# Transposing the gated values of narrow expert slots on VectorE, and moving the wide slot beside slots of two groups

## The chip, the cores and the metric

The kernel runs on one core of a Trainium2 chip. The time is device microseconds (us) of one execution of the whole program; the numbers compared are medians of several runs. TensorE (PE in the profile) multiplies, VectorE (DVE) and ScalarE (ACT) work on elements, SyncE (SP) starts the DMA transfers that bring the weights from the chip's memory.

## The reference, cut to what matters

Two layers of an encoder trunk on 256 tokens of width 1024, in float32. The second layer ends in a mixture of eight experts, each a gated two-layer network of inner width 3584, of which every token uses two:

```python
def swiglu(h, w_gate, w_up, w_down):
    return (jax.nn.silu(h @ w_gate) * (h @ w_up)) @ w_down

def moe_swiglu(h, w_router, b_router, w_gate, w_up, w_down):
    ...
    top_val, top_idx = lax.top_k(logits, TOP_K)
    top_w = jax.nn.softmax(top_val, axis=-1)
    ...
    for e in range(N_EXPERTS):
        out = out + combine[:, e:e + 1] * swiglu(t, w_gate[e], w_up[e], w_down[e])
```

The change lies in these experts alone. Everything ahead of them (the first layer, and the attention and convolution of the second) is the same program in both kernels.

## The kernel before, in words

**Slots.** Expert 0 has slot 0; the other seven experts are sorted by how many tokens chose them, and slots 1 to 7 take them in that order. A slot has room for a fixed number of groups of 32 tokens, `CAPS`: 3, 4, 3, 3, 3, 2, 2, 2. Slot 1, with four groups (128 tokens), is called wide, the others narrow. Tokens that find no room would be worked off by `rest` behind the end, a loop that runs only if there are any.

**Units.** Each slot goes through its expert's inner width in seven chunks of 512. One chunk of one slot is a unit: `gu_mm` multiplies the slot's tokens with the chunk's gate and up weights into `ps_gu`, ScalarE and VectorE form `mh` = silu(gate) * up (lines 1120 and 1123), `h_T` transposes `mh` to `hT`, and `dn_mm` multiplies it with the chunk's down weights, adding to the slot's `ps_d`. The transposition is there because the down product sums over the inner width, which must lie across partitions.

**Order.** Slots stand in two lanes, `LANES`, and units alternate between them; lane 0 starts three units ahead (`STAGGER`). The order is written out by hand under `tc.manual_schedule()`: each engine gets its instructions in the order in which the loop over `units` issues them. For unit n the loop issues `gu_mm` of unit n, then `dn_mm` of unit n-1 (`pend`), then `h_T` of unit n, so that `hT` is read only after the next unit's gate and up product. When a slot ends, `gated` and `combine` add its result to `macc`; two units ahead of a slot's start, `slot_pick` and `dispatch` gather its tokens (`ps_g`, `ps_w`).

**Narrow and wide.** A narrow unit multiplies in plain float32 straight from the loaded weights: for each group four products of 32 rows run beside each other in TensorE's columns (`streams`, line 1089). The wide unit splits each loaded half of a chunk into an upper and a lower part, `hi` on ScalarE (line 140) and `lo` on VectorE (line 148), and makes three products for each (`mm3`, lines 254 to 256). The splits are issued by `ahead`, some units before they are used.

**Loads and buffers.** A unit loads six transfers of 1024 KB (`load`, line 131): four of gate and up weights, two of down weights. They go through SyncE's queue in the order of `plan`, and each waits until its buffer has been read. The pool `raw` has nine buffers of this size. Where no wide chunk is near in the plan, the three `hi` and three `lo` buffers serve as load buffers too (in `need`), fifteen in all:

```python
if i >= first_gu and not any(n_ for _, n_ in plan[i - 6:i + 3]):
    at = m % 15
    return ((rawp, "raw", G), (hip, "hi", G), (lop, "lo", G))[(at >= 9) + (at >= 12)]
return rawp, "raw", G
```

Of the kernel before, what the change touches and what calls it, by code (L numbers as in the profile page):

```python
# [9 lines left out]
F32 = mybir.dt.float32  # L10
F32R = mybir.dt.float32r
I32 = mybir.dt.int32
U32 = mybir.dt.uint32
AF = mybir.ActivationFunctionType
ALU = mybir.AluOpType
AX = mybir.AxisListType

P = 128
# [16 lines left out]
SPARE4 = (1, 6, 8)  # L35
EARLY = 7
CAPS = (3, 4, 3, 3, 3, 2, 2, 2)
LANES = (0, 2, 1, 3), (5, 4, 6, 7)
STAGGER = 3
NR = NE - 1  # L40
EPS = 1e-6
# [12 lines left out]
def kernel(ctx, tc, x, cvec, wada, bada, wga, wqkv, wout, wfgu, wfd, wfd2,  # L54
                      wmgu, wmd, cols, bias, wrt, brt, out):
    nc = tc.nc
# [10 lines left out]
    def bank(name):  # L67
        return pb.tile([P, 512], F32, tag="b", name=name)

    def accbank(name):  # L70
        return pacc.tile([P, 512], F32, tag="acc", name=name)
# [3 lines left out]
    def sized(tag):  # L75
        def f(name, shape, dt=F32):
            return pools["wk"].tile(shape, dt, tag=tag, name=name, bufs=bufs[tag])
        return f

    a8, a4, a2 = sized("a8"), sized("a4"), sized("a2")  # L80
# [23 lines left out]
    ident = const.tile([P, P], F32, name="ident")  # L104
# [17 lines left out]
    def load(ap, n=4096, mk=lambda s: (rawp, "raw", G)):  # L122

        raw = []
        for h in range(n // G):
            src = ap[h] if isinstance(ap, list) else ap[:, h * G:h * G + G]
            pool, tag, w = mk(h)
            raw.append([])
            for o_ in range(0, G, w):
                r = pool.tile([P, w], F32, tag=tag, name="raw", bufs=bufs.get(tag))  # L130
                nc.sync.dma_start(r, src[:, o_:o_ + w])
                raw[-1].append(r)
        return raw
# [29 lines left out]
    first_gu = len(plan)  # L163
    runs = [[(e, c) for e in lane for c in range(N_DN)] for lane in LANES]
    units = runs[0][:STAGGER]
    for u in zip(runs[0][STAGGER:], runs[1]):
        units += u
    units += runs[1][-STAGGER:]
    after = {e: n for lane in LANES for e, n in zip(lane, lane[1:])}
    order = {0: 0}  # L170
# [736 lines left out]
    def moe(acc, g_bc, mm, A, B, AW, bw):  # L907
# [95 lines left out]
        def pick(col, n=P):  # L1003

            pm = a2("pm", [P, 2, NT, P])
            for t in range(NT):
                nc.vector.tensor_scalar(pm[:, 1, t, 0:n], iota_f[:, 0:n], col(t), y[t], op0=ALU.is_equal,
                                        op1=ALU.mult)
            for t in range(NT):
                nc.vector.tensor_scalar(pm[:, 0, t, 0:n], iota_f[:, 0:n], col(t), None, op0=ALU.is_equal)  # L1010
            return pm
# [5 lines left out]
        def gather(pm, n, put):  # L1017

            for q in range(2):
                ps = bank("ps_g").rearrange("p (j s) -> p j s", j=4)  # L1020
                f = a2("xf", [P, 4, P])
                for j in range(4):
                    k = 4 * q + j
                    for t in range(NT):
                        nc.tensor.matmul(ps[:, j, 0:n], x_sb[:, t, k * P:(k + 1) * P], pm[:, 1, t, 0:n],  # L1025
                                         start=t == 0, stop=t == NT - 1)
                for j in range(4):
                    k = 4 * q + j
                    nc.scalar.activation(f[:, j, 0:n], ps[:, j, 0:n], AF.Identity, scale=A[:, k:k + 1],
                                         bias=B[:, k:k + 1])  # L1030
                put(slice(4 * q, 4 * q + 4), f[:, :, 0:n])
# [93 lines left out]
            return hm  # L1125

        def h_T(hm, g, split=False):
            ps = bank("ps_hT").rearrange("p (a s) -> p a s", a=4)
            for t in range(g):
                nc.tensor.transpose(ps[:, t, :], hm[:, t, :], ident)  # L1130
            if split:
                hT = [a2(n, [P, g, P], F32R) for n in ("hThi", "hTlo")]
                nc.scalar.activation(hT[0], ps, AF.Copy)
                nc.vector.tensor_tensor(hT[1], ps, hT[0].bitcast(F32), op=ALU.subtract)
            else:
                hT = a2("hT", [P, g, P])
                nc.scalar.activation(hT, ps[:, 0:g, :], AF.Copy)  # L1137
            return hT

        def dn_mm(e, c, hT):  # L1140
# [67 lines left out]
        def rest(e):  # L1208

            pm = pick(lambda t: posm[:, t, 0:1])  # L1210
            xg = a8("xr", [P, KT, P])
            gather(pm, P, lambda js, f: nc.scalar.activation(xg[:, js, :], f, AF.Copy))
            ps = bank("ps_w")
            for t in range(NT):
                nc.tensor.transpose(ps[:, t * P:(t + 1) * P], pm[:, 0, t, :], ident)
            for t in range(NT):
                nc.tensor.matmul(ps[:, 2 * P:2 * P + 1], pm[:, 0, t, :], comb[:, t, 0:1], start=t == 0,
                                 stop=t == NT - 1)
            pT = a2("pmT", [P, NT, P])
            nc.scalar.activation(pT.rearrange("p t s -> p (t s)"), ps[:, 0:2 * P], AF.Copy)  # L1220
            ws = sm.tile([P, 1], F32, tag="ws", name="ws")
            nc.vector.tensor_copy(ws, ps[:, 2 * P:2 * P + 1])
            acc = [accbank(f"ps_x{hf}") for hf in range(2)]

            def own(w, c):
                return [r for r, in load(w[bass.ds(e, 1), c].rearrange("o p n -> (o p) n"))]

            for c in range(N_DN):
                pss = [bank(f"ps_gr{b}") for b in range(2)]
                for b in range(2):  # L1230
                    for s, r in enumerate(own(wmgu, 2 * c + b)):
                        for i in range(4):
                            k = 4 * s + i
                            nc.tensor.matmul(pss[b], xg[:, k, :], r[:, 512 * i:512 * i + 512], start=k == 0,
                                             stop=k == KT - 1)
                hm = a2("mh", [P, 4, P])
                for b in range(2):
                    v = pss[b].rearrange("p (u j s) -> p j u s", j=2, u=2)
                    sg = a2("sg", [P, 2, P])
                    nc.scalar.activation(sg, v[:, :, 0, :], AF.Silu)  # L1240
                    nc.vector.tensor_tensor(hm[:, 2 * b:2 * b + 2, :], v[:, :, 1, :], sg, op=ALU.mult)
                hT = h_T(hm, 4)
                for hf, r in enumerate(own(wmd, c)):
                    for k in range(4):
                        nc.tensor.matmul(acc[hf], hT[:, k, :], r[:, 512 * k:512 * k + 512], start=c == 0 and k == 0,
                                         stop=c == N_DN - 1 and k == 3)
            for hf in range(2):
                sl = slice(hf * 512, hf * 512 + 512)
                f = a4("yg", [P, 512])
                nc.vector.scalar_tensor_tensor(f, acc[hf], ws, g2_bc[:, sl], op0=ALU.mult, op1=ALU.mult)  # L1250
                for t in range(NT):
                    ps = bank("ps_sc")
                    nc.tensor.matmul(ps, pT[:, t, :], f, start=True, stop=True)
                    nc.vector.tensor_tensor(macc[:, t, sl], macc[:, t, sl], ps, op=ALU.add)
            for v in (posm, comb):
                nx = sm.tile([P, NT, NE], F32, tag="nx", name="nx", bufs=2)
                nc.vector.tensor_copy(nx[:, :, 0:NE - 1], v[:, :, 1:NE])
                nc.vector.tensor_copy(nx[:, :, NE - 1:NE], v[:, :, 0:1])
                nc.vector.tensor_copy(v, nx)
# [33 lines left out]
        with tc.manual_schedule():  # L1293
# [6 lines left out]
            for n, (e, c) in enumerate(units):  # L1300
# [4 lines left out]
                elif n == STAGGER - 1:  # L1305
                    nxt = LANES[1][0]
                else:
# [8 lines left out]
                hm = gu_mm(e, between)  # L1316
                if n == 1:
# [5 lines left out]
                    ps = bank("ps_g2")  # L1323
# [15 lines left out]
                if n + 1 < len(units) and wide(units[n + 1][0]):  # L1339
                    ahead(2)  # L1340
                pend = e, c, h_T(hm, CAPS[e], wide(e))
                if nxt is not None:
                    disp[nxt] = dispatch(nxt, pm)
# [8 lines left out]
        with tc.If(over > 0):  # L1352
            nc.vector.tensor_tensor(posm, posm, own_room[:, None, :].to_broadcast([P, NT, NE]), op=ALU.subtract)
            for again in range(2):
                with tc.For_i(0, NE, 1) as e:
                    rest(e)
                nc.vector.tensor_scalar(posm, posm, float(-P), None, op0=ALU.add)
            for hf in range(2):
                store(hf)
# [152 lines left out]
```

## Time and profile before

| what | value |
|---|---|
| three runs | 1418.91, 1425.69, 1429.92 us (median 1425.69) |
| the profiled execution | 1421.24 us, its span 1419.2 us |
| TensorE, matmul | busy 1349.9 us, 95% of the span |
| VectorE, ScalarE | busy 565.3 us (40%) and 398.4 us (28%) |
| granted TensorE clock, mean | 0.987 |
| memory read | 470.01 MB, 332 GB/s over the span |

The span is from the first to the last instruction of the profiled execution. Shares of busy time are means over stages that differ: from 519 us on the experts run, and everything else stands ahead of that. In the windows below, one row is one stretch of time; its last number is the rate at which the weights arrived.

### The profile page before, as it was taken

What the parts mean: (1) busy time and instruction counts of PE and PEld (TensorE: products, weight loads), DVE (VectorE), ACT (ScalarE), POOL (GpSimd) and SP (SyncE); (2) the same over time, 40 slices, a digit from 0 to 9 for tenths busy, and PEclk for the clock granted to TensorE, in tenths of its full rate; (3) what the DMA queues carried; (4) which work ended last, traced back from release to release, by engine and by line L of the source; (5) the groups of instructions that cost most, each with busy time, mean ns of one, the idle gap of its engine ahead of it and who ended that gap; (6) DMA issues with size and microseconds to landing.
All of it is one profiled execution on the core that took longest, in us unless ns stands there. A gap on an engine that the chain in (4) does not pass through costs nothing.

```text
span 1419.2 us, 38942 instructions
## 1 busy us (share of the span) xinstructions
PE 1349.9 (95%) x17604; PEld 973.1 (69%) x17604; DVE 565.3 (40%) x1025; ACT 398.4 (28%) x635; POOL 3.0 (0%) x17
## 2 busy tenths in 40 slices
PE   4998899999899999999999999999999999999886
PEld 4877699999697686657666656677667766665453
DVE  3597677777689651000100100354455430010011
ACT  3335444433456330101001001334333420100000
POOL 0000000000000000000000000000000000000000
PEclk9999999999999999999999999999999999999998
DMA  9963787878551579899999995989898999999995
GB/s 383 418 243 123 263 308 273 305 272 307 172 205 45 206 292 369 342 417 417 417 417 417 417 417 223 396 350 362 327 379 346 397 417 417 417 417 417 417 418 202
DMA packets 66379, 473.64 MB, mean 334 GB/s; under 512 B 7840, under 2 KB 7968, under 8 KB 9248
## 3 DMA queue, kind: packets, MB, share of 16 engines
q1 hardware_dynamic: 66208, 471.09, 83.3%
q8 instruction: 140, 2.29, 0.6%
q14 instruction: 31, 0.25, 0.0%
HBM read 470.01 MB, written 1.05 MB: 332 GB/s over the span
## 4 chain that ended last, share of the span: by engine, by line
PE 77%; DMA 13%; DVE 5%; ACT 3%; issue 1%; SPq 0%; DVEq 0%; ACTq 0%
PE ps_gu L1089 23%; PE ps_d L1089 13%; DMA raw<-in_wmgu 6%; DMA raw<-in_wmd 6%; PE ps_ga L256 4%; PE ps_ga L254 4%; PE ps_ga L255 4%; PE ps_g L1025 2%; PE ps_y L708 2%; PE ps_gu L256 2%; PE ps_gu L254 2%; PE ps_gu L255 2%; DVE cv L544 2%; PE ps_ada L308 1%; DVE lo L148 1%; PE ps_hT L1130 1%
## 5 line engine op out<-in xcount | busy, mean ns | idle before, releaser
L1089 PE MATMUL ps_gu<-raw,xn 128*32 128x256 f32 x8064 | 450.2, 380 | 4.1 <-DMA raw<-in_wmgu 3.9
L1089 PEld LDWEIGHTS ps_gu<-raw,xn 128*32 128x32 f32 x8064 | 269.1, 110 | 169.2 <-DMA raw<-in_wmgu 7.8
L148 DVE TENSOR_TENSOR lo<-raw,hi 128x2048 fp32r<-128x2048 f32 x99 | 225.5, 2289 | 84.7 <-ACT hi L140 82.0
L1123 DVE TENSOR_TENSOR mh<-ps_gu,sg 128x256 f32<-128x256 f32 (+1 forms) x91 | 32.7, 382 | 547.2 <-ACT sg L1120 547.2
L1089 PE MATMUL ps_d<-raw,hT 128*32 128x256 f32 x4032 | 232.3, 381 | 8.0 <-DMA raw<-in_wmd 7.5
L140 ACT ACTIVATE hi<-raw 128x2048 fp32r<-128x2048 f32 x99 | 188.3, 1912 | 107.2 <-PE ps_ga L256 43.0
L1089 PEld LDWEIGHTS ps_d<-raw,hT 128*32 128x32 f32 x4032 | 133.7, 110 | 96.6 <-DMA raw<-in_wmd 9.9
L1120 ACT ACTIVATE sg<-ps_gu 128x256 f32<-128x256 f32 (+1 forms) x91 | 32.0, 352 | 426.3 <-PE ps_gu L1089 380.7
L254 PE MATMUL ps_ga<-hThi,lo 128*128 128x256 f32 x480 | 137.5, 287 | 7.6 <-ACT hThi L446 7.6
L256 PE MATMUL ps_ga<-hTlo,hi 128*128 128x256 f32 x480 | 136.9, 285 | 0.8 <-DVE hTlo L451 0.8
L255 PE MATMUL ps_ga<-hThi,hi 128*128 128x256 f32 x480 | 136.3, 284 | 0.0
L254 PEld LDWEIGHTS ps_ga<-hThi,lo 128*128 128x128 f32 x480 | 92.9, 194 | 8.7 <-ACT hThi L446 8.4
L256 PEld LDWEIGHTS ps_ga<-hTlo,hi 128*128 128x128 f32 x480 | 92.4, 192 | 1.4 <-DVE hTlo L451 1.4
L255 PEld LDWEIGHTS ps_ga<-hThi,hi 128*128 128x128 f32 x480 | 92.4, 193 | 0.2
L544 DVE SCALAR_TENSOR_TENSOR cv<-zp,cols_sb,cv 128x256 f32<-128x256 f32 x206 | 85.4, 477 | 0.0
L1137 ACT ACTIVATE hT<-ps_hT 128x384 f32<-128x384 f32 (+1 forms) x49 | 21.8, 445 | 221.4 <-PE ps_hT L1130 221.4
L347 DVE SCALAR_TENSOR_TENSOR ada_acc<-raw,cs,ada_acc 128x512 f32<-128x512 f32 x63 | 47.2, 749 | 1.2
L256 PE MATMUL ps_gu<-lo,xg 128*128 128x512 f32 x112 | 44.3, 396 | 1.3 <-DVE lo L148 1.3
L254 PE MATMUL ps_gu<-hi,xg 128*128 128x512 f32 x112 | 44.8, 400 | 0.0
L255 PE MATMUL ps_gu<-hi,xg 128*128 128x512 f32 x112 | 44.3, 396 | 0.0
L308 PE MATMUL ps_ada<-raw,crep 128*32 128x128 f32 x960 | 34.4, 302 | 7.4 <-DMA raw<-in_wada 7.1
L308 PEld LDWEIGHTS ps_ada<-raw,crep 128*32 128x32 f32 x960 | 29.2, 121 | 11.2 <-issue 8.3
(263 smaller groups left out, 1310.1 us busy)
## 6 DMA issues: line engine op xcount, KB each, us to landing
raw<-in_wmgu SPq DMA_DIRECT2D x222, 1024.0 KB, 13.9
raw<-in_wmd SPq DMA_DIRECT2D x111, 1024.0 KB, 14.3
raw<-in_wada SPq DMA_DIRECT2D x48, 1024.0 KB, 6.2
raw<-in_wfgu SPq DMA_DIRECT2D x22, 1024.0 KB, 6.0
raw<-in_wqkv SPq DMA_DIRECT2D x12, 1024.0 KB, 6.6
raw<-in_wfd SPq DMA_DIRECT2D x11, 1024.0 KB, 6.5
raw<-in_wga SPq DMA_DIRECT2D x8, 1024.0 KB, 10.6
raw<-in_wout SPq DMA_DIRECT2D x8, 1024.0 KB, 7.7
```

Source lines behind the costliest of these rows:

```text
L140: nc.scalar.activation(hi[:, i * w:(i + 1) * w], r, AF.Copy)
L148: nc.vector.tensor_tensor(lo[:, w], r, hi[:, w].bitcast(F32), op=ALU.subtract)
L254: nc.tensor.matmul(o_, a[1], b[0], start=first, stop=False)
L255: nc.tensor.matmul(o_, a[0], b[0], start=False, stop=False)
L256: nc.tensor.matmul(o_, a[0], b[1], start=False, stop=last)
L308: nc.tensor.matmul(ps[32 * g:32 * g + 32, 0:P], crep[:, j, :], w(j)[:, g * P:(g + 1) * P], start=j == 0, stop=j == KT - 1)
L347: nc.vector.scalar_tensor_tensor(accs[ch], ws[ch](j), cs[:, j:j + 1], accs[ch], op0=ALU.mult, op1=ALU.add)
L544: nc.vector.scalar_tensor_tensor(cv[:, a, :], zp[:, a, i:i + S], cw[:, a, i:i + 1], cv[:, a, :], op0=ALU.mult, op1=ALU.add)
L708: nc.tensor.matmul(acc[t][hf], yf[:, k, t * P:(t + 1) * P], w(k // 2, 2 * (k % 2) + hf), start=k == 0, stop=False)
L1089: nc.tensor.matmul(ps[t // 2][32 * j:32 * j + 32, t % 2], x(t), w(j), start=first and t % 2 == 0, stop=last, skip_group_check=True)
L1120: nc.scalar.activation(sg[:, 2 * b:2 * b + m, :], v[:, 0:m, 0, :], AF.Silu)
L1123: nc.vector.tensor_tensor(hm[:, 2 * b:2 * b + m, :], v[:, 0:m, 1, :], sg[:, 2 * b:2 * b + m, :], op=ALU.mult)
```

## The change: what it does

```diff
-LANES = (0, 2, 1, 3), (5, 4, 6, 7)
+LANES = (0, 1, 2, 3), (5, 6, 4, 7)
...
         def h_T(hm, g, split=False):
+            if not split:
+
+                hT = a2("hT", [P, g, 4, 32])
+                v = hm.rearrange("p t (q s) -> p t q s", q=4)
+                for q in range(4):
+                    for j in range(4):
+                        nc.vector.transpose(hT[32 * q:32 * q + 32, :, j], v[32 * j:32 * j + 32, :, q])
+                return hT.rearrange("p t j s -> p t (j s)")
             ps = bank("ps_hT").rearrange("p (a s) -> p a s", a=4)
             for t in range(g):
                 nc.tensor.transpose(ps[:, t, :], hm[:, t, :], ident)
-            if split:
-                hT = [a2(n, [P, g, P], F32R) for n in ("hThi", "hTlo")]
-                nc.scalar.activation(hT[0], ps, AF.Copy)
-                nc.vector.tensor_tensor(hT[1], ps, hT[0].bitcast(F32), op=ALU.subtract)
-            else:
-                hT = a2("hT", [P, g, P])
-                nc.scalar.activation(hT, ps[:, 0:g, :], AF.Copy)
+            hT = [a2(n, [P, g, P], F32R) for n in ("hThi", "hTlo")]
+            nc.scalar.activation(hT[0], ps, AF.Copy)
+            nc.vector.tensor_tensor(hT[1], ps, hT[0].bitcast(F32), op=ALU.subtract)
             return hT
```

In the narrow units, the two or three transposes on TensorE and ScalarE's copy out of PSUM go. In their place VectorE transposes each group's 128x128 values as sixteen blocks of 32x32: block (j, q) goes from partitions 32j to partitions 32q, one instruction for all groups of the slot, so sixteen instructions a unit whether it has two groups or three. The wide slot keeps its transposes on TensorE. `rest` gets the old transposes written out in its own body. The lanes become 0, 1, 2, 3 and 5, 6, 4, 7: slot 1 follows slot 0 and runs beside the end of slot 5 and the beginning of slot 6; slots 2, 3 and 4 come later.

TensorE, two narrow units (slot 5's down product on `ps_d_6035` or `ps_d_6091`, then the next unit of slot 5), before:

```order
L1089 MATMUL ps_gu_5924<-raw,xn 32x256 x4
L1089 MATMUL ps_d_6035<-raw,hT 32x256 x32
L1130 MATMUL ps_hT<-ident,mh 128x128 x3
L1089 MATMUL ps_gu_6078<-raw,xn 32x256 x64
L1089 MATMUL ps_d_5319<-raw,hT 32x256 x8
```

and with the change:

```order
L1089 MATMUL ps_gu_5980<-raw,xn 32x256 x4
L1089 MATMUL ps_d_6091<-raw,hT 32x256 x32
L1089 MATMUL ps_gu_6145<-raw,xn 32x256 x64
L1089 MATMUL ps_d_5330<-raw,hT 32x256 x8
L1089 MATMUL ps_d_5331<-raw,hT 32x256 x4
```

The three transposes between one unit's down product and the next unit's gate and up product are gone. VectorE in a pair of a narrow and a wide unit (`lo` are the splits, `mh` the gated values, `hTlo` the wide unit's), before:

```order
L148 TENSOR_TENSOR lo<-raw,hi 128x2048 x2
L1123 TENSOR_TENSOR mh<-ps_gu_9548,sg 128x256
L1123 TENSOR_TENSOR mh<-ps_gu_9549,sg 128x128
L148 TENSOR_TENSOR lo<-raw,hi 128x2048 x4
L1123 TENSOR_TENSOR mh<-ps_gu_9708,sg 128x256
L1123 TENSOR_TENSOR mh<-ps_gu_9709,sg 128x256
L1134 TENSOR_TENSOR hTlo<-ps_hT,hThi 128x512
```

and with the change, where the narrow slot has two groups:

```order
L148 TENSOR_TENSOR lo<-raw,hi 128x2048 x2
L1123 TENSOR_TENSOR mh<-ps_gu_7150,sg 128x256
L148 TENSOR_TENSOR lo<-raw,hi 128x2048 x2
L1134 STREAM_TRANSPOSE hT<-mh 32x2x32 x16
L148 TENSOR_TENSOR lo<-raw,hi 128x2048 x2
L1123 TENSOR_TENSOR mh<-ps_gu_7286,sg 128x256
L1123 TENSOR_TENSOR mh<-ps_gu_7287,sg 128x256
L1141 TENSOR_TENSOR hTlo<-ps_hT,hThi 128x512
```

The sixteen transposes stand between the splits of the wide unit's first two halves and those of its last two. ScalarE at such a pair, before (beside slot 6):

```order
L140 ACTIVATE hi<-raw 128x2048 x2
L1120 ACTIVATE sg<-ps_gu_10695 128x256
L1120 ACTIVATE sg<-ps_gu_10696 128x256
L1133 ACTIVATE hThi<-ps_hT 128x512
L140 ACTIVATE hi<-raw 128x2048 x2
L1120 ACTIVATE sg<-ps_gu_10817 128x256
L140 ACTIVATE hi<-raw 128x2048 x2
L1137 ACTIVATE hT<-ps_hT 128x256
L140 ACTIVATE hi<-raw 128x2048 x2
L1120 ACTIVATE sg<-ps_gu_10944 128x256
```

and with the change:

```order
L140 ACTIVATE hi<-raw 128x2048 x2
L1120 ACTIVATE sg<-ps_gu_7150 128x256
L140 ACTIVATE hi<-raw 128x2048 x4
L1120 ACTIVATE sg<-ps_gu_7286 128x256
L1120 ACTIVATE sg<-ps_gu_7287 128x256
L1140 ACTIVATE hThi<-ps_hT 128x512
```

The copy `hT` no longer stands between the splits.

## Rows read from the trace of the kernel before

**Rows 1.** The page: the chain that ended last, its line by engine.

```profile
PE 77%; DMA 13%; DVE 5%; ACT 3%; issue 1%; SPq 0%; DVEq 0%; ACTq 0%
```

**Rows 2.** Windows: us, busy us of PE, PEld, DVE, ACT, POOL; PEclk, DMA share, GB/s.

```profile
519.00:588.00 69.00, 67.10 (x1178) 48.50 (x1178) 11.09 (x46) 10.23 (x25) 0.00 (x0) 1.00 0.89 358
588.00:858.00 270.00, 270.00 (x4903) 169.33 (x4902) 22.93 (x62) 27.14 (x70) 0.00 (x0) 1.00 1.01 416
858.00:900.00 42.00, 42.00 (x729) 26.49 (x732) 2.72 (x7) 6.92 (x18) 0.00 (x0) 1.00 0.64 250
900.00:932.00 32.00, 30.66 (x391) 21.03 (x385) 15.00 (x16) 10.27 (x11) 0.00 (x0) 1.00 0.85 336
932.00:1048.00 116.00, 114.54 (x1352) 79.90 (x1340) 56.21 (x49) 50.85 (x51) 0.00 (x0) 1.00 0.90 359
1048.00:1136.00 88.00, 88.00 (x833) 65.97 (x833) 44.94 (x37) 36.85 (x38) 0.00 (x0) 0.96 0.94 379
1136.00:1209.00 73.00, 73.00 (x1171) 45.54 (x1168) 13.96 (x22) 11.17 (x20) 0.00 (x0) 1.00 1.01 417
1209.00:1398.00 189.00, 177.72 (x3090) 103.73 (x3089) 15.72 (x35) 14.84 (x37) 0.00 (x0) 0.99 1.01 414
```

**Rows 3.** The chain in order of time, end of the program: start us, us, what.

```profile
1377.01 21.23 DMA raw<-in_wmd
...
1402.83 4.20 PE ps_d L1089 x64
```

**Rows 4.** The chain, one pair of narrow units (slots 0 and 5).

```profile
600.92 10.50 PE ps_gu L1089 x192
611.42 3.45 PE ps_d L1089 x64
614.87 0.48 PE ps_hT L1130 x3
615.35 7.04 PE ps_gu L1089 x128
...
627.94 2.06 PE ps_gu L1089 x33
```

**Rows 5.** SyncE timeline before the wide slot: start us, us, what.

```profile
852.59 31.02 SPq L131 DMA_DIRECT2D raw<-in_wmgu  x4
...
889.04 10.73 SPq L131 DMA_DIRECT2D raw<-in_wmgu  x4
```

**Rows 6.** The chain, a wide unit beside a three-group unit.

```profile
925.76 5.32 PE ps_d L1089 x96
...
959.50 5.32 PE ps_d L1089 x96
```

**Rows 7.** The chain, a wide unit beside a two-group unit.

```profile
1069.91 3.59 PE ps_d L1089 x64
...
1098.36 3.59 PE ps_d L1089 x64
```

**Rows 8.** VectorE timeline in a wide unit: start us, us, what, [idle before].

```profile
946.94 2.29 DVE L148 TENSOR_TENSOR lo<-raw,hi 128x2048 fp32r<-128x2048 f32 x1 [0.27 <-ACT hi L140]
950.67 4.50 DVE L148 TENSOR_TENSOR lo<-raw,hi 128x2048 fp32r<-128x2048 f32 x2 [1.45 <-ACT hi L140]
```

**Rows 9.** TensorE timeline in the same unit: its first matmul.

```profile
948.06 0.48 PE L254 MATMUL ps_gu<-hi,xg 128*128 128x512 f32 x1
```

**Rows 10.** VectorE timeline: simple operations issued back to back.

```profile
966.68 0.53 DVE L1007 TENSOR_SCALAR pm<-iota_f,rt,ny 128x64 f32<-128x64 f32 x2
967.12 0.41 DVE L1010 TENSOR_SCALAR pm<-iota_f,rt 128x64 f32<-128x64 f32 x2
```

**Rows 11.** VectorE groups of one shape each, 519 to 1411 us.

```profile
L1007 DVE TENSOR_SCALAR pm<-iota_f,rt,ny 128x96 f32<-128x96 f32 x6 | 1.7, 324 | 0.0
```

**Rows 12.** TensorE timeline: a wait and what followed.

```profile
1047.97 0.50 PE L1195 MATMUL ps_sc<-yhi,pmT 32*128 32x256 f32 x3 [1.46 <-DVE mh L1123]
```

**Rows 13.** Window with the granted clock after that wait.

```profile
1050.00:1056.00 6.00, 6.00 (x15) 4.65 (x15) 3.49 (x3) 0.78 (x1) 0.00 (x0) 0.53 1.01 426
```

More of the change, by code (lines that the diff above doesn't have):

```diff
@@ L1241, in rest @@
                     nc.vector.tensor_tensor(hm[:, 2 * b:2 * b + 2, :], v[:, :, 1, :], sg, op=ALU.mult)
-                hT = h_T(hm, 4)
+                ps = bank("ps_hT").rearrange("p (a s) -> p a s", a=4)
+                for k in range(4):
+                    nc.tensor.transpose(ps[:, k, :], hm[:, k, :], ident)
+                hT = a2("hT", [P, 4, P])
+                nc.scalar.activation(hT, ps, AF.Copy)
                 for hf, r in enumerate(own(wmd, c)):
```

## The prediction

> **What bounds the kernel now.** I read the page's chain first. It gives TensorE 77% and transfers 13% [rows 1], which looks like a kernel that any saving on TensorE would shorten. But that is a share over stages, so I went on to the windows over the expert stage, and there the column to follow is the last one. From 1209 to 1398 us, the weights arrive at 414 GB/s with a DMA share of 1.01, while TensorE is busy for 177.7 of 189 us [rows 2]. The end of the chain agrees: it passes through a down-weight transfer up to 1398 us, then a last down product of 4.2 us, and the output [rows 3]. The last 200 us are paced by the weight stream. In such a kernel an early microsecond counts only if it lets the stream run when it would have stood still. So I take 414 GB/s as what the stream can do and read from each window how much of it was lost, as length times (414 minus its rate) over 414 [rows 2]:
>
> 519 to 588 us: 69 x 56/414 = 9.3 us; 858 to 900: 42 x 164/414 = 16.6; 900 to 932: 32 x 78/414 = 6.0; 932 to 1048: 116 x 55/414 = 15.4; 1048 to 1136: 88 x 35/414 = 7.4. That is 54.7 us. The windows 588 to 858 and 1136 to 1209, at 416 and 417 GB/s, give back 1.3 and 0.5. So about **53 us** of stream time are lost, and this is all that the change can win in the expert stage; from the last load's arrival on, nothing changes.
>
> **Why the stream stands still.** One unit loads six transfers of 1024 KB, 6.29 MB. At 414 GB/s a transfer takes 2.53 us and a pair of units 30.4 us. Where TensorE needs longer for a pair, the buffers fill and the loads wait; where it needs less, it eats the lead.
>
> - A pair of slots 0 and 5 (three and two groups) takes 600.92 to 627.94 us, 27.0 us [rows 4]: under 30.4.
> - A wide unit beside a three-group unit takes 925.76 to 959.50 us, 33.7 us [rows 6]: 3.3 us over, in the three pairs where slot 1 stands beside slot 4.
> - A wide unit beside a two-group unit takes 1069.91 to 1098.36 us, 28.4 us [rows 7]: under.
> - Just ahead of the wide slot, four loads take SyncE 31.0 us, against 10.7 a little later [rows 5]. Narrow units can use fifteen buffers, and near wide units only nine are left, so a lead of six transfers, 15.2 us of the stream, must be eaten first. Slots 2 and 4, three groups each, run just before it and let the lead fill up. This is the 16.6 us of the window 858 to 900.
>
> **The reordering.** Slot 1 now begins when slot 0 ends, at the twelfth unit instead of the 26th, and stands beside slots 5 and 6 only, two groups each. All seven of its pairs are of the 28.4 us kind. Ahead of it run four pairs of slots 0 and 5, which eat lead (below, 4.2 us each, 17 us in all, or nearly seven transfers), so there is little to shed at the switch. The three-group slots 2, 3 and 4 move behind the wide slot and meet in pairs (2 with 4, 4 with 3) of 2 x (10.5 + 1.5 x 3.45) = 31.4 us without transposes [rows 4], close to the stream's 30.4. No load is added, and their count on SyncE's queue is the same.
>
> **The transposes on TensorE.** A narrow unit loses three or two of them, with 0.48 us on the chain for three [rows 4]; two thirds of it, 0.32, is my estimate for two. A pair of slots 0 and 5 falls from 27.0 to 26.2 us. Where the stream is the limit this buys nothing: it only moves TensorE's idle time. It helps in the first three units, 3 x 0.48 = 1.4 us, and in the pairs of three-group units. ScalarE also loses the copy that stood between two weight splits and waited until TensorE had got to the transposes.
>
> **The sixteen on VectorE.** No row shows this operation. The nearest rows are simple operations of 64 and 96 columns: two follow each other in 0.44 us, 0.22 each, the next two in 0.41 with their end, so some 0.16 apart [rows 10]; one alone of 96 columns lasts 0.324 us [rows 11]. I take 0.22 because issue one behind another is what sixteen independent ones will do; the bounds are 0.16 and 0.32. Nothing bounds an unseen operation from above with certainty, so a dearer one is a rival. Sixteen then take 3.5 us (2.6 to 5.2). Beside narrow neighbours this hides: the product that reads them is issued after the other lane's down product and a further gate/up product, 3.45 + 7.04 = 10.5 us at least [rows 4], and VectorE is busy for 22.9 of 270 us there [rows 2].
>
> Beside the wide slot it doesn't hide by itself. VectorE's queue holds, between the splits for the wide unit's first two halves and those for its last two, the sixteen transposes, and TensorE waits for the latter. In the unit at 948.06 us [rows 9] the third half's first product comes 24 products later. The 48 of the unit end at 959.50 us, where the next down product starts [rows 6], so they are 11.4/48 = 0.24 us apart, and the third half begins at 953.8 us; its first product on a lower part is the third, at 954.2. The split it needs is ready at 950.67 + 2.25 = 952.9, so there are 1.3 us of slack, and VectorE had been idle for 1.45 us before it [rows 8]. Of 3.5 us therefore 3.5 - 1.45 - 1.3 = 0.8 us become a wait of TensorE. The pair: 28.4 less 0.2 for two transposes, plus 0.8, is **29.0 us**, still under 30.4. Up to 0.31 us a transpose the stream covers it; past that each further 0.1 us costs 1.6 us a pair, 11 us over seven pairs.
>
> A page of the Trainium skill speaks against this step: VectorE: DVE Perf Modes, "The three transpose paths" and the rules behind it, advise TensorE for a 128x128 transpose and name VectorE's 32x32 blocks useful for some layouts only, with 311 ns for a 128x128 tile of bf16. No run here shows that figure. If each of the sixteen cost as much, the sum would stand at the very edge of what the stream covers, and hardly change.
>
> **What remains lost.** In the first window 9.3 - 1.4, 8 us. At the switch I keep the 6.0 us of the window 900 to 932 (the first wide unit beside slot 0's combine) and 6 of the 16.6, since one of the nine buffers comes free only when its own turn has been read, however empty the others are: 12 us (bounds 0 and 22.6). In the seven wide pairs 1 us each for splits that hold a buffer, 7 us (0 to 14). Together 27 of 53, so the **gain is 26 us** (bounds 8 and 45).
>
> The profiled execution took 1421.24 us, with 1419.2 of span; minus 26 it is 1395. It lies 4.4 us under the median of the three runs, 1425.69, and against that the forecast is **1400 us**.
>
> **Rivals.**
>
> - *Transposes of 0.35 to 0.5 us.* VectorE then binds the wide pairs. At 0.42 us, 0.11 too dear, 12 of the 26 us are gone: 1412. For it: 32 partitions are used by each, and I know no row for it. Against: all rows of this size are under 0.33 us [rows 10, 11].
> - *Slower.* The same place, much dearer: at 0.7 us sixteen take 11.2, a wide pair 28.2 + 11.2 - 2.75 = 36.7 us, 6.3 over the stream, 44 over seven pairs, less 26: 1444. The gain is used up at 0.31 + 26/112 = 0.54 us, and it decides by over 1% from 0.67. Beside narrow units 11.2 us would also pass the cover of 10.5.
> - *The clock.* After a wait of 1.46 us [rows 12] the granted clock fell to 0.53 for 1050 to 1056 us [rows 13], mostly the lower of its two levels (1.2 for 2.4 GHz), which lost 6 x 0.47 = 2.8 us. With a stream-bound TensorE there are more such waits. One drop in each wide pair makes 31.8 us of 29.0, 1.4 over the stream, 10 in all: 1410. Against: in 200 us of a stream-bound tail the clock is 0.99 [rows 2]. (The Trainium skill, TensorE: Matmul & The Clock Gate, "Why this matters for your kernels", warns of idle gaps between bursts for this reason; the tail, with its short waits, hardly shows it.)
> - *The change doesn't do what it says at the switch.* If the loss there is not lead but the nine buffers, all 22.6 us stay: 1411.
> - *More:* if the switch and the wide pairs lose nothing, the gain is 45 us: 1381.
>
> **How the numbers follow.** One per cent, 14 us, is about what a measurement of this kernel can tell from no change (the three runs span 11 us). Chances: the forecast, 1390 to 1409 us, 0.58; dearer transposes 0.16, somewhat over half of it past 1411.6; the clock 0.06 and the switch 0.07, both close to that bound; slower 0.08; more than forecast 0.05. Faster by over 1%: 0.58 + 0.07 + 0.03 + 0.05 + 0.05 = 0.78; slower 0.08; within, the rest, 0.14. The range from 1388 to 1420 leaves out the slower case, part of the largest gain and the dearest of the transposes.
>
> **What would show it.** Expected after: sixteen transposes in 3 to 4 us; the stream at 410 GB/s or more from about 600 us on but for a dip of some 12 us near 700, where the wide slot begins; wide pairs 29 to 31 us apart; no stretch under 300 GB/s around 860; TensorE's idle time spread through the stage, with waits for transfers in place of transposes. The forecast is wrong if wide pairs are over 32 us apart (transposes or clock), or if the dip at the switch is as deep as before.

## The result, and the profile after

| | before | after |
|---|---|---|
| median of 4 runs each, same chip | 1423.65 us (1418.91 to 1429.92) | 1404.99 us (1402.64 to 1409.61) |
| the profiled execution | 1421.24 us | 1405.31 us (span 1403.6) |
| first expert product begins | 519.21 us | 522.03 us |
| TensorE, VectorE, ScalarE busy | 1349.9, 565.3, 398.4 us | 1327.8, 764.3, 377.2 us |

The ratio is 0.987, with a 95% interval from 0.9822 to 0.9918: 1.3% faster, 18.7 us by the medians and 15.9 between the two profiled executions. The forecast was 1400 us, a gain of 26. TensorE has lost 22 us of work and VectorE has taken on 200 us, so the page's shares alone would tell little; the line of its chain, by engine, which answers to [rows 1]:

```profile
PE 77%; DMA 9%; DVE 8%; ACT 4%; issue 2%; SPq 0%; DVEq 0%; ACTq 0%
```

TensorE holds the same 77%, transfers fell from 13% to 9%, and VectorE rose from 5% to 8%. The windows say more. These are after's, cut at its own stages, with the columns of [rows 2]; the wide slot now runs from about 690 to 910 us:

```profile
519.00:588.00 69.00, 67.61 (x1264) 44.40 (x1267) 28.17 (x110) 10.93 (x27) 0.00 (x0) 1.00 0.86 338
588.00:660.00 72.00, 72.00 (x1294) 53.69 (x1290) 25.58 (x97) 6.92 (x18) 0.00 (x0) 1.00 1.01 415
660.00:720.00 60.00, 54.68 (x731) 36.07 (x724) 30.35 (x54) 16.86 (x16) 0.00 (x0) 0.94 0.84 323
720.00:900.00 180.00, 170.57 (x1666) 124.08 (x1668) 114.46 (x173) 77.72 (x75) 0.00 (x0) 0.99 0.97 391
900.00:1180.00 280.00, 279.37 (x5065) 176.66 (x5058) 104.64 (x346) 24.87 (x58) 0.00 (x0) 1.00 1.01 415
1180.00:1384.00 204.00, 197.08 (x3616) 124.38 (x3612) 77.55 (x278) 12.20 (x32) 0.00 (x0) 1.00 0.99 405
```

The long hole of [rows 2] (250 GB/s, then 336, 359 and 379 between 858 and 1136 us) has become 60 us at 323 and 180 at 391. As in the prediction, the stream time lost is length times (414 minus the rate) over 414: 12.7 us in the first row, 13.2 from 660 to 720, 10.0 from 720 to 900, 4.4 in the last, and 0.9 given back in the two others, 39.4 in all against some 53 before. The chain at the end confirms the gain without this arithmetic:

```profile
1361.23 21.38 DMA raw<-in_wmd
...
1382.65 8.81 PE ps_d L1089 x124
```

The last load arrives at 1361.23 + 21.38 = 1382.6 us, where before it was 1398.2 [rows 3]: 15.6 us earlier, and what follows it takes as long as it did.

**Narrow pairs.** The chain of a pair of slots 0 and 5, which answers to [rows 4]:

```profile
600.68 10.36 PE ps_gu L1089 x192
...
626.58 5.55 PE ps_gu L1089 x101
```

From 600.68 to 626.58 it is 25.9 us, against 27.0; no transposition stands on TensorE, and no wait stands in its place.

**Wide pairs.** The chain from one narrow down product of 64 beside the wide slot to the next:

```profile
705.23 3.59 PE ps_d L1089 x64
...
735.19 3.59 PE ps_d L1089 x64
...
768.40 3.59 PE ps_d L1089 x64
...
899.44 3.59 PE ps_d L1089 x64
```

Two successive rows of `ps_d` lie a pair apart, as in [rows 7]: 29.96 us from 705.23 to 735.19, where nothing else stands in the pair, and 33.2 to 768.40, where a gather (`ps_g`, at 752.21) stands in the pair. The next four take 29.9, 35.1, 30.8 and 35.2 us: three of the six hold a gather or a combination, and together they take 194.2 us (705.23 to 899.44), 32.4 on the mean. VectorE's timeline inside the first plain pair (start us, us, what, idle before):

```profile
721.23 2.29 DVE L148 TENSOR_TENSOR lo<-raw,hi 128x2048 fp32r<-128x2048 f32 x1 [0.17 <-ACT hi L140]
723.43 3.98 DVE L1134 STREAM_TRANSPOSE hT<-mh 32x64 f32<-32x64 f32 x16
727.45 4.50 DVE L148 TENSOR_TENSOR lo<-raw,hi 128x2048 fp32r<-128x2048 f32 x2
```

The sixteen transposes stand between two splits as the order said. They take 3.98 us, 0.25 each, and the idle time that was there [rows 8] is gone. What TensorE waits for the split behind them, in us, times and longest:

```profile
PE ps_gu L256 <- DVE lo L148: 9.7, 6, 2.3
PE ps_gu L254 <- ACT hi L140: 3.7, 1, 3.7
```

The first row is 1.6 us each, in six of the seven wide units (in the unit with the gather at 752.21 there is none); the trace of before has one such wait of 1.3 us. The second row is in the first wide unit: there the sixteen transposes stand in VectorE's queue ahead of `yg`, slot 0's result, ScalarE's `yhi` waits for that, and the next split `hi` is issued behind `yhi`. The trace of before has no such wait.

### The profile page after: what moved, and what is told of

Its sections match the earlier page's. It is cut to its first block, busy times and chain, and to the rows that moved or that the text cites. A ratio compares the mean times of both kernels' runs of the same rounds, so it can differ in the third digit from the quotient of the medians.

```text
span 1403.6 us, 39376 instructions
## 1 busy us (share of the span) xinstructions
PE 1327.8 (95%) x17478; PEld 971.8 (69%) x17478; DVE 764.3 (54%) x1809; ACT 377.2 (27%) x586; POOL 3.0 (0%) x17
## 4 chain that ended last, share of the span: by engine, by line
PE 77%; DMA 9%; DVE 8%; ACT 4%; issue 2%; SPq 0%; DVEq 0%; ACTq 0%
PE ps_gu L1089 26%; PE ps_d L1089 13%; DMA raw<-in_wmd 4%; DMA raw<-in_wmgu 4%; PE ps_ga L256 4%; PE ps_ga L254 4%; PE ps_ga L255 4%; DVE lo L148 3%; PE ps_g L1025 2%; PE ps_y L708 2%; DVE cv L544 2%; PE ps_ada L308 2%; ACT hi L140 1%; DVE hT L1134 1%; PE ps_f L254 1%
## 5 line engine op out<-in xcount | busy, mean ns | idle before, releaser
L1089 PEld LDWEIGHTS ps_gu<-raw,xn 128*32 128x32 f32 x8064 | 275.4, 110 | 164.6 <-DMA raw<-in_wmgu 4.7
L1134 DVE STREAM_TRANSPOSE hT<-mh 32x96 f32<-32x96 f32 (+1 forms) x784 | 200.1, 255 | 13.1 <-PE ps_bc L373 0.2
L1089 PEld LDWEIGHTS ps_d<-raw,hT 128*32 128x32 f32 x4032 | 137.7, 110 | 88.4 <-DMA raw<-in_wmd 5.9
L308 PE MATMUL ps_ada<-raw,crep 128*32 128x128 f32 x960 | 34.7, 303 | 7.5 <-DMA raw<-in_wada 7.2
```

Of the source, the lines that this page charges most:

```text
L308: nc.tensor.matmul(ps[32 * g:32 * g + 32, 0:P], crep[:, j, :], w(j)[:, g * P:(g + 1) * P], start=j == 0, stop=j == KT - 1)
L1089: nc.tensor.matmul(ps[t // 2][32 * j:32 * j + 32, t % 2], x(t), w(j), start=first and t % 2 == 0, stop=last, skip_group_check=True)
L1134: nc.vector.transpose(hT[32 * q:32 * q + 32, :, j], v[32 * j:32 * j + 32, :, q])
```

## The experiments

Two theories stood against each other. **S**, the prediction's: the weight stream sets the time, and the order of the slots, by letting it stand still less, gives the gain, while the transposes give little or take some back. **T**: the gain is TensorE's own time (22 us less work, near the 18.7 gained), and the order matters little. Each run was timed in turn with the kernel before on the same chip; the ratio to it stands with its 95% interval. The first four share 17 runs of before (median 1421.69 us), the last four 11 on another chip (1422.59).

**1. The lanes alone.** Narrow units keep their transposes on TensorE and ScalarE's copy; the diff is against the kernel before.

```diff
-LANES = (0, 2, 1, 3), (5, 4, 6, 7)
+LANES = (0, 1, 2, 3), (5, 6, 4, 7)
```

> New lanes, transposes still on TensorE. Theory S (the stream sets the time, and the new order lets it stand still less): nearly the whole gain stays, 14 to 20 us under the kernel before (ratio 0.986 to 0.990), with no transfer gap of 15 us ahead of the wide slot. Rival T (what counts is TensorE's freed time, 28 x 0.48 + 21 x 0.32 = 20 us over 49 narrow units): within 4 us of the kernel before.

Measured: 1406.08 us (1398.29 to 1408.05), ratio 0.987 [0.9843, 0.9898]. As far as the intervals can tell, this is all of after's gain (its ratio is 0.987 too), with all of TensorE's transposes in place. So T falls as the account of this gain; what TensorE's freed time is worth in the new lanes, run 5 shows. The page's chain by engine, windows, pairs beside the wide slot, and two units of the three-group slots:

```profile
PE 90%; DVE 4%; ACT 3%; DMA 2%; issue 1%; SPq 0%; ACTq 0%; DVEq 0%
```

```profile
660.00:720.00 60.00, 58.58 (x895) 37.45 (x887) 20.17 (x21) 15.60 (x17) 0.00 (x0) 1.00 0.86 345
720.00:900.00 180.00, 178.66 (x1772) 130.60 (x1766) 95.67 (x79) 82.63 (x83) 0.00 (x0) 0.99 0.99 405
1180.00:1386.00 206.00, 206.00 (x3712) 129.22 (x3708) 18.81 (x46) 18.99 (x48) 0.00 (x0) 1.00 0.98 398
```

```profile
709.71 3.59 PE ps_d L1089 x64
...
738.17 3.59 PE ps_d L1089 x64
...
895.79 3.59 PE ps_d L1089 x64
```

```profile
1044.73 5.18 PE ps_d L1089 x96
...
1060.88 5.18 PE ps_d L1089 x96
```

A plain wide pair takes 28.46 us, as in [rows 7], and six pairs 186.1 us (31.0 on the mean), so the stream keeps 405 GB/s there against after's 391. In the tail it is the other way round: TensorE is busy throughout, three-group units are 16.15 us apart, and the stream gets 398 GB/s. Over the experts TensorE waits for no transfer, and transfers hold 2% of the chain where before they held 13% [rows 1]: with the new lanes and its transposes, TensorE and not the stream sets the pace of the tail. After's chain at the same units:

```profile
1045.83 5.18 PE ps_d L1089 x96
...
1061.37 5.18 PE ps_d L1089 x96
```

15.54 us. So the transposes on VectorE cost 8 us beside the wide slot (194.2 less 186.1) and save 0.6 us in each unit of the three-group slots that meet; over the fourteen units of slot 4 and of slots 2 and 3 beside it that is some 8 us, and the two nearly cancel.

**2. The transposes alone,** in the old lanes.

```diff
-LANES = (0, 1, 2, 3), (5, 6, 4, 7)
+LANES = (0, 2, 1, 3), (5, 4, 6, 7)
```

> Old lanes, transposes on VectorE. Theory S: within 5 us of the kernel before, perhaps 1 to 2 us slower: what TensorE saves comes back as stream time lost ahead of and beside the wide slot, where the sixteen transposes of 0.27 us (4.3 us) stand between the splits. Rival T: 15 to 20 us faster than before, most of the change's gain.

Measured: 1426.59 us (1423.1 to 1432.0), ratio 1.0031 [1.0015, 1.0046]. It takes TensorE's transposes away and gains nothing, which T can't explain. The two windows of the switch and a wide pair beside three groups:

```profile
858.00:900.00 42.00, 42.00 (x755) 25.51 (x745) 15.21 (x41) 5.71 (x8) 0.00 (x0) 1.00 0.84 330
900.00:932.00 32.00, 26.12 (x285) 18.10 (x288) 17.19 (x30) 9.30 (x8) 0.00 (x0) 0.89 0.67 256
```

```profile
921.13 5.32 PE ps_d L1089 x96
...
956.80 5.32 PE ps_d L1089 x96
```

The window up to 900 us improved on [rows 2] (330 for 250 GB/s), the next one got worse (256 for 336), and the pair takes 35.7 us against 33.7 [rows 6].

**3. Twice the transposes ahead of wide units,** to price them: each of the sixteen is issued twice, with the same values written, in the seven units that stand just ahead of a wide one.

```diff
-nc.vector.transpose(hT[32 * q:32 * q + 32, :, j], v[32 * j:32 * j + 32, :, q])
+for _ in range(twice):
+    nc.vector.transpose(hT[32 * q:32 * q + 32, :, j], v[32 * j:32 * j + 32, :, q])
...
-pend = e, c, h_T(hm, CAPS[e], wide(e))
+beside = n + 1 < len(units) and wide(units[n + 1][0])
+pend = e, c, h_T(hm, CAPS[e], wide(e), 2 if beside else 1)
```

> The changed kernel, with the sixteen transposes issued twice (same values) in the seven narrow units just ahead of a wide one. Theory S with VectorE's chain at its edge there: each wide pair gets some 4 us longer, less half a microsecond of room, 7 x 3.5 = 24 us over the changed kernel, about 1429 us. Rival (the transposes are hidden beside the wide slot too, and the stream alone sets the pair): no change, within 4 us of the changed kernel.

Measured: 1442.48 us (1440.23 to 1443.71), ratio 1.0131 [1.0106, 1.0156], 37.5 us over after. Pairs on the chain, the waits for the split, and the window:

```profile
707.74 3.59 PE ps_d L1089 x64
...
744.54 3.59 PE ps_d L1089 x64
...
936.88 3.59 PE ps_d L1089 x64
```

```profile
PE ps_gu L256 <- DVE lo L148: 32.1, 7, 6.6
```

```profile
720.00:940.00 220.00, 187.13 (x1725) 135.10 (x1727) 138.49 (x269) 79.68 (x76) 0.00 (x0) 0.91 0.84 332
```

Seven waits of 4.6 us on the mean where after has six of 1.6, and a plain pair of 36.8 us where after has 30.0. Six pairs take 229.1 us (38.2 on the mean, 5.8 over after's), and these 34.9 us over after's 194.2 are nearly the whole difference: the stream covered none of it, and more was lost than the 24 us expected. Only the pair with the gather (744.54 to 779.28, 34.7 us) is little longer than after's 33.2; there TensorE has the gather's products to do. Sixteen more transposes take 4.3 us (8.30 for 3.98), so part of the 6.8 us of the plain pair is the clock, which was granted at 0.91 over these 220 us, against 0.99 in after's window.

**4. The transposes behind the wide unit's last splits.** Same lanes and the same sixteen instructions, but in the units ahead of a wide one they are issued between pieces of the wide unit's product, once its last splits are issued.

```diff
+nonlocal pend
...
+if pend and pend[3] is not None:
+    pend = *pend[:2], h_T(pend[3], CAPS[pend[0]]), None
...
-pend = e, c, h_T(hm, CAPS[e], wide(e))
+if n + 1 < len(units) and wide(units[n + 1][0]):
+    pend = e, c, None, hm
+else:
+    pend = e, c, h_T(hm, CAPS[e], wide(e)), None
```

> The changed kernel, but in the seven narrow units just ahead of a wide one the transposes are issued behind the wide unit's last splits. Theory S with VectorE's chain: TensorE's waits for a split in the middle of the wide units (9.7 us over six) go, pairs fall from 30 to 28.4 us, and the time falls by 4 to 9 us against the changed kernel, to about 1399. Rival (buffers and the stream bind the wide pairs, not the transposes): within 2 us of the changed kernel.

Measured: 1391.62 us (1385.73 to 1394.36), ratio 0.9775 [0.9746, 0.9803], 13.4 us under after. Pairs, waits and windows:

```profile
698.88 3.59 PE ps_d L1089 x64
...
727.12 3.59 PE ps_d L1089 x64
...
883.74 3.59 PE ps_d L1089 x64
```

```profile
PE ps_gu L256 <- DVE lo L148: 1.6, 1, 1.6
```

```profile
660.00:720.00 60.00, 58.39 (x751) 39.52 (x744) 35.98 (x56) 21.46 (x18) 0.00 (x0) 1.00 0.90 362
720.00:900.00 180.00, 178.66 (x1845) 130.94 (x1844) 119.63 (x191) 77.86 (x77) 0.00 (x0) 0.99 1.00 407
```

One wait is left of six, the plain pair is 28.2 us, six pairs take 184.9 us (30.8 on the mean, 9.3 less than after's), and the windows rise to 362 and 407 GB/s from 323 and 391. The place in VectorE's queue was the cost, not the operation. The gain was larger than the 4 to 9 us expected: 9.3 us stand in the six pairs, and some 5.6 ahead of them, where the first wide unit's wait of 3.7 us is gone as well (from the first expert product to the first of these rows, 177.6 us against after's 183.2).

**5. TensorE's transposes beside the wide slot only,** VectorE's elsewhere.

```diff
+if split == 2:
+    hT = a2("hT", [P, g, P])
+    nc.scalar.activation(hT, ps[:, 0:g, :], AF.Copy)
+    return hT
...
-pend = e, c, h_T(hm, CAPS[e], wide(e))
+beside = n + 1 < len(units) and wide(units[n + 1][0])
+pend = e, c, h_T(hm, CAPS[e], 2 if beside else wide(e))
```

> The changed kernel, but the seven narrow units just ahead of a wide one keep their transposes and the copy on TensorE and ScalarE. If VectorE's chain between the splits was the only cost beside the wide slot, this is as good as issuing them late: within 4 us of that run's 1391.6 us. Rival (what helped there was that ScalarE lost the copy, which stood between two splits): it stays near 1400 us or above.

Measured: 1388.35 us (1385.35 to 1389.27), ratio 0.9753 [0.9724, 0.9782], the fastest; its interval overlaps that of run 4. Pairs:

```profile
696.07 3.59 PE ps_d L1089 x64
...
724.53 3.59 PE ps_d L1089 x64
```

28.46 us, and six in 184.6: the rival falls, since the copy on ScalarE stands between the splits here. The time is 34 us under before. Against run 1 this kernel differs only in the other 42 narrow units, whose transposes leave TensorE (and ScalarE's copy with them), and the ratio falls from 0.987 to 0.9753, by some 17 us. That is about TensorE's whole time for them, an estimated 28 x 0.48 + 14 x 0.32 = 17.9 us [rows 4]. So T was wrong on what made the change faster, but its term is real: once the new lanes keep the stream running, TensorE is what the tail waits for (run 1), and there its freed time counts.

**6. Twice the transposes in the other 42 narrow units** (again the same values twice), none doubled ahead of wide ones; the diff is against run 3.

```diff
-pend = e, c, h_T(hm, CAPS[e], wide(e), 2 if beside else 1)
+pend = e, c, h_T(hm, CAPS[e], wide(e), 2 if not beside else 1)
```

> The changed kernel, with the sixteen transposes issued twice (same values) in all narrow units that do not stand just ahead of a wide one, 42 of 49. Theory: the next unit's products cover 7 to 9 us, no change, within 3 us of the changed kernel (1405). Rival (they are on the path everywhere): 42 x 4.1 = 172 us more.

Measured: 1402.88 us (1398.2 to 1406.85), ratio 0.9862 [0.9835, 0.989]: no difference from after. VectorE's timeline:

```profile
607.31 9.43 DVE L1135 STREAM_TRANSPOSE hT<-mh 32x96 f32<-32x96 f32 x32
...
617.95 8.36 DVE L1135 STREAM_TRANSPOSE hT<-mh 32x64 f32<-32x64 f32 x32
```

Transposes of 9.43 and 8.36 us follow the gated values here, and in the whole stage TensorE waits once for `hT`, 2.8 us at the very end. The second sixteen, which cost 37.5 us in seven units, cost nothing in 42.

**7. The wide slot as early, but beside three groups.** Slot 4 takes slot 5's place at the head of its lane.

```diff
-LANES = (0, 1, 2, 3), (5, 6, 4, 7)
+LANES = (0, 1, 2, 3), (4, 5, 6, 7)
```

> The changed kernel with lanes (0, 1, 2, 3) and (4, 5, 6, 7): the wide slot stands as early as in the change, but behind pairs of three-group slots and beside slot 4 (three groups) for three units, then slot 5. Theory (a full lead ahead of the switch, and pairs over the stream's 30.4 us while it is full, are lost; the same work behind a drained lead is not): 25 to 40 us over the changed kernel, and 10 to 20 over the kernel before, with a gap of some 15 us in the transfers ahead of the wide slot, near 680 us. Rival (an early place of the wide slot is what helps): close to the changed kernel, within 8 us.

Measured: 1445.91 us (1442.87 to 1452.43), ratio 1.0159 [1.0127, 1.019], 41 us over after and 23 over before, each a little more than expected. SyncE ahead of the wide slot, and the windows:

```profile
682.44 20.48 SPq L131 DMA_DIRECT2D raw<-in_wmd  x2
```

```profile
660.00:720.00 60.00, 54.75 (x900) 33.80 (x899) 25.26 (x65) 13.42 (x20) 0.00 (x0) 0.98 0.70 275
720.00:930.00 210.00, 200.81 (x2207) 142.84 (x2208) 116.42 (x166) 79.43 (x79) 0.00 (x0) 0.97 0.83 328
```

Ahead of the wide slot now run pairs of three-group units, which by the prediction's account leave the lead full, and two loads take 20.5 us to issue; the windows fall to 275 and 328 GB/s; a wide pair beside slot 4 takes 37.2 us (730.06 to 767.27). Early is no gain in itself: what counts is which slots run ahead of the wide one and beside it. The run doesn't separate these two.

**8. The old lanes with late transposes,** run 4 with run 2's edit.

```diff
-LANES = (0, 1, 2, 3), (5, 6, 4, 7)
+LANES = (0, 2, 1, 3), (5, 4, 6, 7)
```

> Old lanes, transposes on VectorE, issued behind the wide unit's last splits in the units ahead of a wide one. Theory: without VectorE's chain the transposes alone do help a little with the old lanes, by some 1.0 us a pair where pairs are over the stream and by a freed ScalarE: 8 to 15 us under the kernel before. Rival (transposes on VectorE are worth nothing by themselves): within 4 us of the kernel before.

Measured: 1410.44 us (1409.15 to 1414.61), ratio 0.9909 [0.9881, 0.9937]. A wide pair beside three groups takes 33.4 us (917.40 to 950.82), against 35.7 in run 2. Well placed, the transposes gain 12 us without the lanes; with the new lanes a further 19 follow (1391.62).

## Why the prediction was right, and where its terms were off

**What sets the time** was right for before and after. The order of the slots carries the gain (run 1: 15.6 us of it, run 2: -4.9 without it), through the windows that the prediction named, and the last load's arrival moved by 15.6 us, as much as the time of the profiled execution. It isn't right for every kernel here: in run 1 TensorE sets the pace of the tail. The prediction said that TensorE's transposes count in the pairs of three-group units, but gave them no price there; run 5 against run 1 puts all 42 units at some 17 us.

**The switch** was right in size, 12 us expected and 13.2 lost, but not in its parts. SyncE's timeline ahead of the wide slot, which answers to [rows 5], and two windows around the first wide unit:

```profile
662.73 15.30 SPq L131 DMA_DIRECT2D raw<-in_wmd  x2
```

```profile
680.00:700.00 20.00, 14.68 (x95) 10.30 (x84) 15.21 (x25) 6.46 (x5) 0.00 (x0) 0.83 0.95 361
700.00:720.00 20.00, 20.00 (x270) 13.68 (x269) 9.75 (x10) 7.50 (x7) 0.00 (x0) 1.00 0.63 233
```

A wait of the queue remains ahead of the wide slot, two loads in 15.3 us where four took 31.0. What it costs is little: from 640 to 680 us the stream still gets 394 GB/s, a loss of 1.9 us, where before lost 16.6 ahead of its wide slot. So the lead had been mostly eaten, as forecast. The loss stands behind 680: 2.6 us up to 700 and 8.7 up to 720, around the first wide unit, where TensorE waits 3.7 us for a split, then 1.6 for the next, and the granted clock is 0.83 (mostly the higher of its two levels, 2.4 GHz, with a stretch of the lower, 1.2). In run 4, without these waits, only 7.5 us are lost from 660 to 720 (362 GB/s), so some 6 of the 13.2 go with the place of the transposes. The prediction had put 6.0 us for the first wide unit and 6 for the buffers ahead of it; that its 12 us came so near is partly luck.

**The transposes' duration** was a little low, inside its bounds. VectorE's groups of one shape over the experts:

```profile
L1134 DVE STREAM_TRANSPOSE hT<-mh 32x96 f32<-32x96 f32 x448 | 120.8, 270 | 7.8 <-PE ps_bc L373 0.2
...
L1134 DVE STREAM_TRANSPOSE hT<-mh 32x64 f32<-32x64 f32 x336 | 79.3, 236 | 5.3
```

236 ns for two groups and 270 for three; issued behind each other, 0.25 us apart instead of 0.22. TensorE's wait was put at 0.8 us and is 1.6: 0.5 of the difference is the duration (4.0 for 3.5 us), the rest is slack, some 0.9 us where the prediction worked out 1.3. So the plain pair is 30.0 us, not 29.0.

**The step that failed** inside a forecast that held is "Up to 0.31 us a transpose the stream covers it". It compared a plain pair with the stream's 30.4 us. But of six wide pairs three hold a gather or a combination, and with these the mean is 31.0 us even with the transposes left on TensorE (run 1). On the mean there was no room, and what VectorE's queue adds to TensorE's waits is lost. The run of pairs shows it from both sides: 1.4 us a pair and 8 over six between run 1 and after, 5.8 a pair and 35 over six between after and run 3. What did cover the transposes, in one pair of the six, was TensorE's own work: with a gather's products ahead of the wide unit's, the pair takes 33.2 us in after and 33.4 in run 1. The trace of before shows the dearer pairs too: the pair behind that of [rows 6] holds a gather and runs from 959.50 to 998.22, 38.7 us. The rows of [rows 6] and [rows 7] were undisturbed, and were used as if they were the mean. With the transposes out of the way, by either road (runs 4 and 5), the change is worth 30 to 34 us, more than the 26 forecast.

The prediction's own sign, wide pairs over 32 us apart, was thus passed by the pairs with a gather or a combination (33.2 to 35.2 us) and not by the others (29.9 to 30.8); and the stream, expected at 410 GB/s or more outside the switch, got 391 beside the wide slot.

**What remains lost** was put at 27 us and is 39.4: 12.7 for 8 in the first window, 13.2 for 12 at the switch, 10.0 for 7 in the wide pairs, and 3.5 net for none elsewhere (the tail's 4.4 less 0.9). The rounding of the rates to whole GB/s allows 2 us either way over this length. Of the first window's excess 2.8 us are a later start: ahead of anything that the change touches, the gather for the first slots took longer, in the chain

```profile
512.63 6.93 PE ps_g L1025 x32
```

against 3.83 us for the same row before, with the clock at the lower of its two levels (1.2 for 2.4 GHz), as a window shows, though TensorE had waited for no more than 0.5 us at a time from 485 us on:

```profile
512.00:517.00 5.00, 4.50 (x21) 4.41 (x22) 2.40 (x13) 1.50 (x4) 0.00 (x0) 0.50 1.01 408
```

The same gather takes 6.9 to 7.0 us in the traces of runs 1 and 7 and 3.83 in those of runs 2 to 6 and 8, whose program is the same up to there, so this is chance and neither theory's.

**The rivals.** Dear transposes: not their price (0.25 us), but their place made the loss that this rival spoke of, and run 3 shows the slower case: its units spend as long on transposes as sixteen of 0.5 us would, and it is 1.3% slower than before, so the point from which this decides lies under the 0.67 us worked out. The clock: no drop in each wide pair, 0.99 over 720 to 900 us, but one at the first wide unit (0.83 above); run 3, with longer waits, does bring it (0.91 over 220 us). The Trainium skill's advice to keep transposes of this size on TensorE (VectorE: DVE Perf Modes, "Rules for kernel authors") holds beside the wide slot by run 5, yet run 4 gets the same time with VectorE, and run 6 shows room for twice as many elsewhere: what decided was the queue and not the operation.

**Left open:** the first window loses between 7 and 14 us from run to run. The three traces with the slow gather lose the most, 12.7 to 13.8 us, and the others 7.2 to 9.8; why the clock falls there in some executions stays open. So does how much of the switch is the nine buffers, since no run changed their number, and whether the wide slot's place or its neighbours count for more (run 7).

## What to carry to other kernels

Where a stream of loads sets the time, compare it with the mean of everything that a stage does, gathers and combinations included, and not with its cleanest step: a cover of 1.4 us (30.4 less 29.0) read from a plain pair was none. Order the work so that light units drain the lead before the buffers shrink, and heavy units have light neighbours; the two together gave 15.6 us here (run 1), and no run separates them. Then look again at what sets the pace: with the order changed, TensorE's time counted in the tail, where it had not before. Work moved to an engine with idle time still costs where it stands in front of something another engine waits for: the same sixteen instructions were free in one place, cost about 13 us in another, and cost nothing there when issued a few instructions later.

## What the runs showed of the hardware

VectorE's transposition of 32 partitions costs 236 ns for 64 columns of float32 and 270 for 96, with 32 of them in 9.43 us back to back (0.29 each) for the larger and 32 in 8.36 (0.26) for the smaller. Waits of TensorE that repeat were dearer than their length: in run 3 the wide units wait 4.6 us on the mean, and the granted clock over the stage falls to 0.91 of the higher level, where waits of 1.6 us left it at 0.99. A plain pair there is 6.8 us longer, for 4.3 us of work put in the way.
